# A softmax-attention stage reordered: products split around the additions, the maxima folded one unit earlier

## The chip, the cores and the metric

The kernel runs on one core of a Trainium2 chip. The metric is the time of one execution on the device in microseconds (us). Three executions of the kernel before took 3257.56, 3263.22 and 3268.09 us, median 3263.22.

## The reference, cut to what matters

One layer of an encoder is computed for two sequences, a prompt of 512 and a sample of 2048 tokens. The part in question is the attention of 8 heads, of 96 columns for queries and keys and 64 for values:

```
s = einsum('bqhd,bkhd->bhqk', q_blk, k_full) * scale
p = softmax(s, axis=-1)
o = einsum('bhqk,bkhd->bqhd', p, v)
```

Before it stand norms and projections, behind it an output projection (`w_out`) and a feed-forward part with a convolution. Everything is to be exact to about single precision.

## The kernel before, in words

Float32 products are made from float16 pairs: a value is split into a high part and a low part, and the large products are summed from pieces. `V` holds the high part, the low part and a column of ones side by side, so that one product also gives the softmax's denominator.

**Units.** The attention is cut into units. A unit of the prompt is one head and 256 queries (two blocks of 128, `nq` = 2) against 4 key tiles, in two PSUM banks; there are 16. A unit of the sample is one head and 128 queries (`nq` = 1) against 16 key tiles, in four PSUM banks of 128 keys x 512 columns (4 tiles x 128 queries); there are 128. Keys lie on the partitions. The scores of a bank stay in PSUM, rotating over seven banks; an eighth, the side bank (`psX`, one buffer, tile `x`), holds small things.

**What a unit does**, by function and line:

- `st_scores` (L939): 12 matmuls for each bank of scores on TensorE.
- `st_max` (L951, for the prompt L954 and L957): VectorE reduces a bank to the maximum over its 4 tiles, per key partition and query.
- `st_fold` (L965): VectorE folds the four banks' maxima into `mx`.
- `st_T` (L981): TensorE transposes `mx` into the side bank, in columns 384 to 512.
- `st_redT` (L989, L992, L995): VectorE reduces the transposed maxima to one per query, `m`, and splits it into a rounded part (bitwise and) and a remainder (subtract) in the small tile `p3`. These last two are called rounding and remainder here.
- `st_rep` (L1003, L1006): TensorE transposes `p3` back into the side bank (replication), ScalarE copies it with a factor of -1 into `mr` (negation).
- `st_r1` (L1015): TensorE adds the negated maxima to the scores of each bank in PSUM (the additions: four short matmuls).
- `st_exp` (L1028): ScalarE takes the exponential of each bank, with a scale `cs` per partition and a bias `ln_shift`, into `pf` (two buffers).
- `st_hi` (L1040 VectorE, L1042 ScalarE): casts of `pf` to float16, `ph`. Bank 0 on ScalarE, bank 1 on VectorE, banks 2 and 3 together on VectorE.
- `st_lo` (L1047): GpSimd subtracts, `pl = pf - ph`, one operation for each bank.
- `st_pv` (L1062, L1063): products with `V` on TensorE, a pair of matmuls for each key tile (16 pairs in a sample unit), in columns 0 to 129 of the side bank. It comes in two parts of 10 and 6 pairs (`PARTS`).
- `st_out` (L1075, L1078): ScalarE copies the sums out; each fourth time GpSimd adds high and low halves. `st_out2` (L1090, L1096): VectorE divides.

**The order** is written out by hand. The framework keeps each engine's instructions in the order of the program (a manual schedule) and sets the semaphores. For each `i` a string of letters is walked through, where `i` is the unit that is just exponentiated: scores and maxima run ahead (units `i+1`, `i+2`), products behind (`i-2`). In the sample:

```
ORDER = "r e0 A L M N P o e1 a T d f l1 b R i c h l0 l2 l3 x y z q"
```

`r` additions, `e0 e1` exponentials of banks 0 to 2 and of 3, `A P` the two parts of the products, `L` scores of bank 3 of unit `i+1`, `a b c` scores of banks 0 to 2 of unit `i+2`, `M x y z` their maxima, `N` fold of unit `i+1`, `T d R` transposes, reduction and replication of unit `i+1`, `h f i` casts, `l0` to `l3` subtractions, `o q` output. `START` and `ORDER2` are the orders for the prompt's units. There, the products go to a bank of the rotation and not to the side bank.

**Beside the units**, every fourth and the following `i` advance `prep_w_out` by one step: it loads `w_out`, finds its greatest absolute value, and splits the weights. The maximum over the partitions is made by GpSimd (`partition_all_reduce`, L840).

Of the kernel before, what the change touches and what calls it, by code (L numbers as in the profile page):

```python
# [19 lines left out]

P = 128
D = 1024
# [26 lines left out]
def encoder(ctx, tc, ins, outs, seq_names=("x_prompt", "x_sample")):  # L49
# [26 lines left out]
    dve.memset(neg_half, -0.5)  # L76
    ln_shift = small([P, 1], "ln_shift")
    dve.memset(ln_shift, LN_SHIFT)
    act.activation(small([P, 1], "warm"), ln_shift, AF.Square)

# [738 lines left out]

    def prep_w_out(raw):  # L820
# [17 lines left out]
        yield  # L838
        amr2 = raw.tile([P, 1], F32, name="amr2", bufs=1)
        pool.partition_all_reduce(amr2, am2[:, 16:17], channels=P, reduce_op=bass_isa.ReduceOp.max)  # L840
        yield
# [51 lines left out]
    with tp("pB", 2) as pB, tp("psX", 1, "right", space=PSUM) as psX, \  # L893
# [49 lines left out]
        def st_max(i, b):  # L943
            u = units[i]
            w = u["w"]
            t0, t1 = u["banks"][b]
            st = u["st"][b]
            if t1 - t0 == 4:
                if b == 0:
                    u["mx4"] = pB.tile([P, 4, P], F32, name=f"mx4_{i}", tag="mx4")  # L950
# [16 lines left out]
        def side_tile(i):  # L967

            if ("x", i) not in state:
                state["x", i] = psX.tile([P, 512], F32, name=f"x_{i}", tag="x")  # L970
            return state["x", i]

        def st_T(i):
            u = units[i]
            xp = side_tile(i - 1)
            old = units[i - 1 - LAG]["nq"] if i > LAG else 1
            u["alone"] = u["nq"] > 1 or old > 1
            u["mrp"] = xp[:, 512 - u["w"]:] if u["alone"] else xp[:, 129:129 + P]
            xp = u["xp"] = xp[:, 512 - u["w"]:]
            for j in range(u["nq"]):  # L980
                pe.matmul(xp[:, j * P:(j + 1) * P], u["mx"][:, j * P:(j + 1) * P], ident, is_transpose=True,  # L981
                          start=u["alone"], stop=True, skip_group_check=True)

        def st_redT(i):
# [3 lines left out]
            m = mc[:, 0:nq]  # L988
            dve.tensor_reduce(m, u["xp"][:, :nq * P].rearrange("p (j k) -> p j k", j=nq), axis=AX.X, op=ALU.max)  # L989
            hi, lo = p3[:, 0:nq, :, 0], p3[:, 0:nq, :, 1]  # L990
# [3 lines left out]
            for j in range(nq):  # L994
                dve.tensor_scalar(out=lo[:, j], in0=mb[:, j], scalar1=p3[:, j, 0, 0:1], scalar2=None,  # L995
                                  op0=ALU.subtract)

        def st_rep(i):
# [3 lines left out]
            for j in range(nq):  # L1002
                pe.matmul(u["mrp"][:, j * P:(j + 1) * P], p3[:, j].rearrange("p a b -> p (a b)"), ident,  # L1003
                          is_transpose=True, start=u["alone"], stop=True, skip_group_check=True)
            mr = pB.tile([P, 256], F32R, name=f"mr2_{i}", tag="mr2")
# [25 lines left out]
        def st_hi(i, b):  # L1031
# [4 lines left out]
            c = cols(u, b)  # L1036
            if b == 2 and len(u["banks"]) == 4:
                c = slice(c.start, cols(u, 3).stop)
            if b in (1, 2):
                dve.tensor_copy(u["ph"][:, c], u["pf"][:, c])  # L1040
            elif b == 0:
                act.activation(u["ph"][:, c], u["pf"][:, c], AF.Copy)  # L1042
# [59 lines left out]

        NU = len(units)
        prep = prep_w_out(pB)
        LAG = 2
        PARTS = [0, 10, 16]
        ps_first = {}
# [11 lines left out]
        def some(fn, k, bs):  # L1119
            if 0 <= k < NU:  # L1120
                for b in bs:
# [7 lines left out]
            e1=lambda i: some(st_exp, i, [3]),  # L1129
            A=lambda i: run(st_pv, i - LAG, 0),  # L1130
            P=lambda i: run(st_pv, i - LAG, 1),
            
            L=lambda i: some(st_scores, i + 1, [3]),
# [4 lines left out]
            u=lambda i: some(st_scores, i + 3, [1]),  # L1138
            v=lambda i: some(st_max, i + 3, [0]),
            w=lambda i: some(st_max, i + 3, [1]),  # L1140
# [4 lines left out]
            N=lambda i: run(st_fold, i + 1),  # L1145
            f=lambda i: some(st_hi, i, [1]),
            h=lambda i: some(st_hi, i, [0]),
            i=lambda i: some(st_hi, i, [2]),
            l0=lambda i: some(st_lo, i, [0]),
# [5 lines left out]
            R=lambda i: run(st_rep, i + 1),  # L1155
            o=lambda i: run(st_out, i - LAG),
            q=lambda i: run(st_out2, i - LAG - 1))
        START = ["a b x y", "a b T d t x u y R", "r e T d t R x y u f l1 h l0",
                 "r e T d t R x y u f l1 h l0", "r e T d A P R x y f l1 h l0 o q"]
        ORDER2 = "r e T d a b x R f l1 y h A P q o l0 c z"  # L1160
        ORDER = "r e0 A L M N P o e1 a T d f l1 b R i c h l0 l2 l3 x y z q"
        for i in range(-2, NU):
            whole = units[min(max(i, 0) + 1, NU - 1)]["nq"] == 1
            for x in (START[i + 2] if i + 2 < len(START) else ORDER if whole else ORDER2).split():
                step[x](i)
# [7 lines left out]
        todo = [(0, 0), (0, 1), (1, 0), (1, 1), (0, 2), (1, 2), (0, 3), (1, 3)]  # L1173
        for i in range(NU, NU + LAG):
            for part in range(2):
                run(st_pv, i - LAG, part)
            run(st_out2, i - LAG - 1)
            run(st_out, i - LAG)
            m = i - NU
# [4 lines left out]
            if m == LAG - 1:  # L1184
                st_out2(NU - 1)
            for x in range(3 * m + 2, 3 * m + 5):
                list(split_w_out(x))
            for t, m in todo[:4]:
                c_mm2(t, m)
            del todo[:4]  # L1190
# [531 lines left out]
```

## Time and profile before

| what | value |
|---|---|
| median of 3 runs (lowest, highest) | 3263.22 us (3257.56, 3268.09) |
| the profiled execution's own time | 3256.74 us |
| its span, first to last instruction | 3254.9 us |
| mean granted clock of TensorE | 0.978 of full speed |
| busy: TensorE, VectorE, ScalarE, GpSimd | 94%, 66%, 43%, 27% of the span |
| first and last additions (L1015) | 358.8 and 1268 us |

Times inside the profile count from the span's first instruction. PE is TensorE's matmul, PEld its weight load, DVE VectorE, ACT ScalarE, POOL GpSimd. A row of the timeline gives start, duration, engine, line, operation, output and inputs, shapes, count, and in brackets the engine's idle time ahead of it and what ended that. A matmul's duration contains its way through the array; the next one begins before it ends. A mark as L1015 is a line of the kernel before.

### The profile page before, as it was taken

How to read it: one execution, taken by the hardware profiler on the slowest of the kernel's cores; microseconds unless marked ns; L12 is line 12 of the kernel's file. 1: busy time of each engine (PE TensorE's matmuls, PEld its weight loads, DVE VectorE, ACT ScalarE, POOL GpSimd, SP SyncE). 2: the span in 40 equal slices, each digit the busy share in tenths (PEclk: the TensorE clock that was granted, in tenths of full speed). 3: DMA queues.
4: the chain of work that ended last, by engine and by line, in shares of the span. 5: the costliest groups of instructions: out<-in, count | busy, mean ns of one | idle time of the engine just before them, and what ended most of it. 6: DMA issues, size and time to landing. Idle time of an engine off the chain costs nothing. (4 is left out here: it accounts for less than half of the span.)

```text
span 3254.9 us, 59928 instructions
## 1 busy us (share of the span) xinstructions
PE 3044.8 (94%) x24601; PEld 1959.7 (60%) x24601; DVE 2161.2 (66%) x4783; ACT 1400.4 (43%) x2863; POOL 875.7 (27%) x825
## 2 busy tenths in 40 slices
PE   6999888888887888999999999999999999999998
PEld 4777577777776776444555555555545555555554
DVE  6677788788887887335777777734357666674333
ACT  4554556556565665223333333433333333333333
POOL 1211467777776775221000000000100000000000
PEclk9999899999998999999999999999999999999999
DMA  3333221201110102576111111311161111113112
GB/s 133 105 108 92 72 50 34 70 5 24 31 22 8 28 4 75 190 220 168 45 47 40 40 39 40 112 36 36 57 150 40 51 41 39 40 38 102 42 38 75
DMA packets 272061, 210.37 MB, mean 65 GB/s; under 512 B 48739, under 2 KB 247722, under 8 KB 271530
## 3 DMA queue, kind: packets, MB, share of 16 engines
q1 hardware_dynamic: 270012, 200.23, 21.1%
q0 software_dynamic: 1440, 5.24, 0.4%
q8 instruction: 193, 3.16, 0.4%
q10 hardware_dynamic: 334, 1.06, 0.1%
q14 instruction: 82, 0.67, 0.1%
HBM read 140.51 MB, written 55.38 MB: 60 GB/s over the span
## 5 line engine op out<-in xcount | busy, mean ns | idle before, releaser
L1288 PE MATMUL up<-h,ws 128*128 128x512 f16 (+1 forms) x6336 | 1146.6, 344 | 7.3 <-DMA h<-h_x_sample 5.9
L1288 PEld LDWEIGHTS <-ws 128*128 128x128 f16 x6336 | 619.9, 98 | 533.3 <-issue 6.1
L1047 POOL TENSOR_TENSOR pl<-pf,ph 128x512 f16<-128x512 f32 x544 | 660.6, 1242 | 239.9 <-DVE ph L1040 197.0
L1387 PE MATMUL dn<-G,wds 128*128 128x512 f16 (+1 forms) x3168 | 579.0, 344 | 0.0
L939 PE MATMUL st<-Q,K 96*128 96x128 f16 (+1 forms) x6336 | 469.4, 225 | 3.3 <-ACT pf L1028 2.1
L1387 PEld LDWEIGHTS <-wds 128*128 128x128 f16 x3168 | 310.0, 98 | 254.2
L939 PEld LDWEIGHTS <-K 96*128 96x128 f16 x6336 | 420.9, 102 | 14.7 <-issue 3.8
L1028 ACT ACTIVATE pf<-st,ln_shift,cs 128x512 f32<-128x512 f32 x544 | 392.7, 774 | 56.6 <-PE st L1015 47.0
L951 DVE TENSOR_REDUCE mx<-st 128x128 f32<-128x512 f32 x512 | 329.3, 684 | 70.3 <-PE st L939 69.5
L1293 ACT ACTIVATE c<-up,ctab 128x511 f32<-128x511 f32 (+3 forms) x264 | 182.1, 699 | 407.4 <-PE up L1288 401.0
L1294 DVE SCALAR_TENSOR_TENSOR c<-up,ctab,c 128x510 f32<-128x510 f32 (+3 forms) x264 | 173.5, 657 | 185.7 <-ACT c L1293 183.0
L1062 PE MATMUL x<-V,ph 128*128 128x129 f16 x2072 | 238.4, 232 | 0.4 <-ACT t L1075 0.4
L1063 PE MATMUL x<-V,pl 128*128 128x65 f16 x2072 | 228.9, 202 | 6.6 <-POOL pl L1047 6.6
L1062 PEld LDWEIGHTS <-ph 128*128 128x128 f16 x2176 | 211.3, 105 | 32.3 <-issue 32.2
L1063 PEld LDWEIGHTS <-pl 128*128 128x128 f16 x2176 | 207.2, 103 | 7.7 <-POOL pl L1047 7.3
L1394 DVE SCALAR_TENSOR_TENSOR yt<-dn,yscB,yt 128x512 f32<-128x512 f32 (+1 forms) x48 | 31.5, 660 | 227.5 <-ACT yt L1393 217.7
L1297 DVE SCALAR_TENSOR_TENSOR c<-up,ctab,c 128x511 f32<-128x511 f32 (+1 forms) x264 | 174.7, 662 | 9.3
L1006 ACT ACTIVATE mr<-x 128x128 fp32r<-128x128 f32 (+1 forms) x143 | 41.2, 288 | 276.0 <-PE x L1003 276.0
L130 ACT ACTIVATE ws<-wr,sF 128x1024 f16<-128x1024 f32 x88 | 96.2, 1138 | 147.0 <-DVE sF L1265 142.0
L1335 POOL PARTITION_ALL_REDUCE imrA<-imxA x2 | 0.7, 374 | 576.9 <-DVE imxA L1333 576.9
L1262 POOL PARTITION_ALL_REDUCE war<-wam x22 | 7.8, 356 | 527.0 <-DVE wam L1260 520.6
L1415 POOL TENSOR_TENSOR y<-y,fng 128x512 f32<-128x512 f32 (+1 forms) x42 | 45.3, 1083 | 384.4 <-ACT yp L1406 349.7
(410 smaller groups left out, 3716.4 us busy)
## 6 DMA issues: line engine op xcount, KB each, us to landing
wr<-in_w_up SPq DMA_DIRECT2D x88, 512.0 KB, 4.9
wd<-in_w_down SPq DMA_DIRECT2D x32, 512.0 KB, 4.3
x_s<-in_x_sample SPq DMA_DIRECT2D x8, 1024.0 KB
xt_Cs<-in_x_sample SPq DMA_DIRECT2D x8, 1024.0 KB, 7.8
x_x_sample<-xt_Cs SPq DMA_DIRECT2D x8, 1024.0 KB, 4.0
h_x_sample<-rows_Cs SPq DMA_DIRECT2D x16, 512.0 KB, 2.7
wd<-in_w_down SPq DMA_DIRECT2D x16, 384.0 KB, 3.5
y<-x_x_sample SPq DMA_DIRECT2D x3, 2048.0 KB, 8.7
```

The source lines that it names most:

```text
L130: act.activation(hi, src, AF.Identity, scale=scale)
L939: pe.matmul(st[:, (t - t0) * w:(t - t0 + 1) * w], kt[:, x, t * P:(t + 1) * P], qt[:, y, u["q0"]:u["q0"] + w], start=n == 0 and t == t0, st ...
L951: dve.tensor_reduce(u["mx4"][:, b, :], st.rearrange("p (t q) -> p q t", q=w), axis=AX.X, op=ALU.max)
L1028: act.activation(u["pf"][:, c], u["st"][b][:, :c.stop - c.start], AF.Exp, bias=ln_shift[:, 0:1], scale=cs[:, 0:1])
L1047: pool.tensor_tensor(out=u["pl"][:, c], in0=u["pf"][:, c], in1=u["ph"][:, c], op=ALU.subtract)
L1062: pe.matmul(op[:, j, 0:129], u["ph"][:, c0:c0 + P], V[:, k0 + t, h, 0:129], start=t == 0, stop=False)
L1063: pe.matmul(op[:, j, 64:129], u["pl"][:, c0:c0 + P], V[:, k0 + t, h, 64:129], start=False, stop=t == nkt - 1)
L1288: pe.matmul(ps[:, :ncol], ws[side][:, k, x, :], ht[:, k, y, :ncol], start=m == 0, stop=m == 3 * KT - 1)
L1293: act.activation(c[:, :n], ps[:, :n], AF.Identity, scale=cw[:, 1, col:col + 1], bias=ctab[:, 3, col:col + 1])
L1294: dve.scalar_tensor_tensor(out=c[:, 1:n], in0=ps[:, 0:n - 1], scalar=cw[:, 0, col:col + 1], in1=c[:, 1:n], op0=ALU.mult, op1=ALU.add)
L1297: dve.scalar_tensor_tensor(out=c[:, 0:j1], in0=ps[:, 1:1 + j1], scalar=cw[:, 2, col:col + 1], in1=c[:, 0:j1], op0=ALU.mult, op1=ALU.add)
L1387: pe.matmul(acc[part][:, :n], w[f // 8][:, f % 8, x, :], G_[0][:, f, y, o:o + n], start=f in (0, NF - 1) and (x, y) == (0, 0), stop=f >= N ...
```

## The change

The sample's unit is reordered, and with it what the side bank holds. The diff, cut to its core:

```diff
-    ln_shift = small([P, 1], "ln_shift")
-    dve.memset(ln_shift, LN_SHIFT)
...
-        pool.partition_all_reduce(amr2, am2[:, 16:17], channels=P, reduce_op=bass_isa.ReduceOp.max)
+        pm = side()[0:1, 256:384]
+        pe.matmul(pm, am2[:, 16:17], ident, is_transpose=True, start=False, stop=True, skip_group_check=True)
+        m1 = raw.tile([1, 1], F32, name="m1", bufs=1)
+        dve.tensor_reduce(m1, pm, axis=AX.X, op=ALU.max)
+        yield
+        pm = side()[:, 256:257]
+        pe.matmul(pm, m1.to_broadcast([1, P]), ident[:1, :1], is_transpose=True, ...)
+        dve.tensor_copy(amr2, pm)
...
+        shift = pB.tile([P, 1], F32, name="shift", bufs=1)
+        dve.reciprocal(shift, cs)
+        dve.tensor_scalar(out=shift, in0=shift, scalar1=LN_SHIFT, scalar2=None, op0=ALU.mult)
...
-                dve.tensor_reduce(u["mx4"][:, b, :], st.rearrange("p (t q) -> p q t", q=w), axis=AX.X, op=ALU.max)
+                dve.tensor_reduce(u["mx2"] if b == 3 else u["mx3"][:, :, b], st.rearrange("p (t q) -> p q t", q=w),
+                                  axis=AX.X, op=ALU.max)
...
-                dve.tensor_reduce(u["mx"][:, 0:P], u["mx4"].rearrange("p b q -> p q b"), axis=AX.X, op=ALU.max)
+                dve.tensor_reduce(u["mx"][:, 0:P], u["mx3"], axis=AX.X, op=ALU.max)
...
+            x = state["x", i] = psX.tile([P, 512], F32, name=f"x_{i}", tag="x")
+            parts = [u["mx"][:, j * P:(j + 1) * P] for j in range(u["nq"])]
+            if u["nq"] == 1:
+                parts.append(u["mx2"])
+            u["xp"], u["mrp"] = x[:, 0:256], x[:, 512 - u["w"]:]
...
-                dve.tensor_scalar(out=lo[:, j], in0=mb[:, j], scalar1=p3[:, j, 0, 0:1], scalar2=None,
-                                  op0=ALU.subtract)
+                dve.tensor_scalar(out=lo[:, j], in0=mb[:, j], scalar1=p3[:, j, 0, 0:1], scalar2=shift[:, 0:1],
+                                  op0=ALU.subtract, op1=ALU.subtract)
...
-            act.activation(u["pf"][:, c], u["st"][b][:, :c.stop - c.start], AF.Exp, bias=ln_shift[:, 0:1],
-                           scale=cs[:, 0:1])
+            act.activation(u["pf"][:, c], u["st"][b][:, :c.stop - c.start], AF.Exp, scale=cs[:, 0:1])
...
-                op = side_tile(i + LAG) if units[min(i + LAG + 1, NU - 1)]["nq"] == 1 else bank(f"op_{i}")
+                op = state["x", i + 2] if i + 2 < NU else bank(f"op_{i}")
...
-        PARTS = [0, 10, 16]
+        PARTS = [0, 8, 16]
...
+            A=lambda i: run(st_pv, i - 1, 0),
+            B=lambda i: run(st_pv, i - 2, 1),
+            F=lambda i: run(st_fold, i + 2),
+            h0=lambda i: run(st_hi, i, 0),
+            h1=lambda i: run(st_hi, i, 1),
+            f1=lambda i: run(st_hi, i, 1, 1, dve),
+            f2=lambda i: run(st_hi, i, 2, 1, dve),
+            f3=lambda i: run(st_hi, i, 3, 1, dve),
...
-        ORDER2 = "r e T d a b x R f l1 y h A P q o l0 c z"
-        ORDER = "r e0 A L M N P o e1 a T d f l1 b R i c h l0 l2 l3 x y z q"
+        ORDER2 = "r e B o T d a b x R f1 l1 y h0 A q l0 c z F"
+        TURN = "r e B o L a M x T d b h0 f1 R y l0 l1 A c z F q"
+        ORDER = "r e0 B L o e1 a M f2 T d b c h0 R h1 l2 l0 l1 A x y z F f3 l3 q"
```

So a unit's products now come in halves of 8 pairs: `A`, behind the unit's next but one replication and into the same side tile, and `B`, behind the additions of the `i` after that. The fold `F` takes three banks and is made one `i` earlier; the fourth bank's maxima `mx2` are transposed by themselves, and the reduction runs over both transposes. `f2` and `f3` cast banks 2 and 3 on VectorE, `h0` and `h1` banks 0 and 1 on ScalarE. The exponential's shift goes into the remainder. The prompt's products go to the side bank too. `TURN` is the order of the one unit between prompt and sample, and the tail behind the last unit is written anew for the split products.

## Rows read from the trace of the kernel before

**Rows 1.** Windows: us, busy PE, PEld, DVE, ACT, POOL, PEclk, DMA share, GB/s.

```profile
358.83:424.92 66.09, 55.55 (x490) 41.75 (x490) 53.36 (x132) 39.11 (x73) 37.39 (x35) 0.85 0.36 86
444.59:1260.80 816.21, 692.78 (x10666) 602.85 (x10664) 674.20 (x1350) 481.26 (x877) 624.77 (x529) 0.95 0.11 26
```

**Rows 2.** Timeline of one sample unit, 849.8 to 856.2 us, all engines.

```profile
849.82 0.51 PE L1015 MATMUL st<-mr,ones 2*128 2x512 f32 x4
850.26 0.23 PE L1062 MATMUL x<-V,ph 128*128 128x129 f16 x1
850.42 2.12 ACT L1028 ACTIVATE pf<-st,ln_shift,cs 128x512 f32<-128x512 f32 x3 [0.36 <-PE st L1015]
...
851.11 0.19 PE L1063 MATMUL x<-V,pl 128*128 128x65 f16 x1
851.25 0.83 PE L939 MATMUL st<-Q,K 96*128 96x128 f16 x12
...
852.11 0.69 DVE L951 TENSOR_REDUCE mx<-st 128x128 f32<-128x512 f32 x1 [0.55 <-PE st L939]
...
852.63 0.28 ACT L1075 ACTIVATE t<-x 128x129 f32<-128x129 f32 x1
852.84 1.06 DVE L965 TENSOR_REDUCE mx<-mx 128x128 f32<-128x512 f32 x1
...
854.04 0.30 PE L981 MATMUL x<-ident,mx 128*128 128x128 f32 x1 [0.77 <-DVE mx L965]
854.38 0.29 DVE L989 TENSOR_REDUCE mc<-x 128x1 f32<-128x128 f32 x1 [0.49 <-PE x L981]
...
855.20 0.33 PE L1003 MATMUL x<-ident,p 128*128 128x128 f32 x1 [0.18 <-DVE p L995]
855.57 0.28 ACT L1006 ACTIVATE mr<-x 128x128 fp32r<-128x128 f32 x1 [1.99 <-PE x L1003]
855.62 4.82 POOL L1047 TENSOR_TENSOR pl<-pf,ph 128x512 f16<-128x512 f32 x4 [1.49 <-DVE ph L1040]
...
856.13 0.50 PE L1015 MATMUL st<-mr,ones 2*128 2x512 f32 x4
```

**Rows 3.** Windows: longest unit, a long one, a usual one; three, then five prompt units.

```profile
1003.88:1019.93 16.05, 8.08 (x90) 7.41 (x88) 5.18 (x11) 3.86 (x8) 9.46 (x9) 0.57 0.00 1
482.44:490.04 7.60, 6.86 (x90) 6.17 (x88) 5.17 (x11) 3.86 (x8) 4.82 (x5) 0.78 0.01 2
490.04:496.35 6.31, 5.35 (x89) 4.63 (x87) 5.17 (x11) 3.85 (x8) 5.50 (x6) 1.00 0.00 0
...
370.81:387.56 16.75, 16.75 (x102) 12.64 (x102) 10.62 (x28) 8.55 (x16) 8.73 (x8) 0.51 0.09 25
391.41:411.70 20.29, 16.53 (x172) 12.55 (x170) 18.15 (x47) 13.11 (x26) 13.25 (x12) 1.00 0.26 71
```

**Rows 4.** Groups by shape, ScalarE, whole span.

```profile
L1028 ACT ACTIVATE pf<-st,ln_shift,cs 128x512 f32<-128x512 f32 x544 | 392.7, 774 | 56.6 <-PE st L1015 47.0 <-POOL pl L1047 9.3
L1393 ACT ACTIVATE yt<-dn,yscA 128x512 f32<-128x512 f32 x32 | 21.9, 686 | 195.5 <-PE dn L1387 195.5
```

**Rows 5.** Groups by shape, VectorE, whole span.

```profile
L989 DVE TENSOR_REDUCE mc<-x 128x2 f32<-128x256 f32 x15 | 6.3, 421 | 9.6 <-PE x L981 9.6
```

**Rows 6.** Timeline of GpSimd, then of VectorE, 362.9 to 365.5 us, a prompt unit.

```profile
362.95 2.26 POOL L1047 TENSOR_TENSOR pl<-pf,ph 128x512 f16<-128x512 f32 x2 [23.37 <-DVE ph L1040]
...
363.59 0.55 DVE L992 TENSOR_SCALAR p<-mc 128x8 int32<-128x8 int32 x1
364.17 1.20 DVE L995 TENSOR_SCALAR p<-mc,p 128x4 f32<-128x4 f32 x2
```

**Rows 7.** Waits of weight loads, 450 to 1250 us: total us, times, longest.

```profile
PEld x L981 <- ACT pf L1028: 105.1, 118, 0.9
```

**Rows 8.** Timeline of TensorE, a prompt unit whose additions begin at 403.64 us.

```profile
404.49 0.41 PE L981 MATMUL x<-ident,mx 128*128 128x128 f32 x2 [0.35 <-DVE mx L954]
```

**Rows 9.** Timeline of GpSimd, 995 to 1020 us.

```profile
1001.50 0.38 POOL L840 PARTITION_ALL_REDUCE amr<-am  x1 [5.93 <-DVE mx L951]
```

More of the change, by code (lines that the diff above doesn't have):

```diff
@@ L76, in encoder @@
     dve.memset(neg_half, -0.5)
-    ln_shift = small([P, 1], "ln_shift")
-    dve.memset(ln_shift, LN_SHIFT)
-    act.activation(small([P, 1], "warm"), ln_shift, AF.Square)
+    act.activation(small([P, 1], "warm"), neg_half[:, 0:1], AF.Square)
     n_scale = [0]
@@ L818, in w_o_part, with prep_w_out @@
         return w_o[:, m, part * 512:part * 512 + 512].bitcast(F16)
-    def prep_w_out(raw):
+    def prep_w_out(raw, side):
         am2 = raw.tile([P, 17], F32, name="am2", bufs=1)
@@ L838, in prep_w_out @@
         yield
+        pm = side()[0:1, 256:384]
[4 more added lines that the diff above has]
+        pm = side()[:, 256:257]
+        pe.matmul(pm, m1.to_broadcast([1, P]), ident[:1, :1], is_transpose=True, start=False, stop=True,
+                  skip_group_check=True)
         amr2 = raw.tile([P, 1], F32, name="amr2", bufs=1)
-        pool.partition_all_reduce(amr2, am2[:, 16:17], channels=P, reduce_op=bass_isa.ReduceOp.max)
-        yield
+        dve.tensor_copy(amr2, pm)
         swo, swo_i = pow2_scale(amr2, 15)
@@ L949, in st_max @@
                 if b == 0:
-                    u["mx4"] = pB.tile([P, 4, P], F32, name=f"mx4_{i}", tag="mx4")
-                dve.tensor_reduce(u["mx4"][:, b, :], st.rearrange("p (t q) -> p q t", q=w), axis=AX.X, op=ALU.max)
+                    u["mx3"] = pB.tile([P, P, 3], F32, name=f"mx3_{i}", tag="mx3")
+                if b == 3:
+                    u["mx2"] = pB.tile([P, P], F32, name=f"mx2_{i}", tag="mx2")
+                dve.tensor_reduce(u["mx2"] if b == 3 else u["mx3"][:, :, b], st.rearrange("p (t q) -> p q t", q=w),
+                                  axis=AX.X, op=ALU.max)
             elif b:
@@ L964, in st_fold @@
                 u["mx"] = pB.tile([P, 256], F32, name=f"mx_{i}", tag="mx")
-                dve.tensor_reduce(u["mx"][:, 0:P], u["mx4"].rearrange("p b q -> p q b"), axis=AX.X, op=ALU.max)
[L967 to L971, printed above, removed]
+                dve.tensor_reduce(u["mx"][:, 0:P], u["mx3"], axis=AX.X, op=ALU.max)
         def st_T(i):
             u = units[i]
[L975 to L982, printed above, removed]
+            x = state["x", i] = psX.tile([P, 512], F32, name=f"x_{i}", tag="x")
[3 more added lines that the diff above has]
+            u["xp"], u["mrp"] = x[:, 0:256], x[:, 512 - u["w"]:]
+            for j, part in enumerate(parts):
+                pe.matmul(u["xp"][:, j * P:(j + 1) * P], part, ident, is_transpose=True, start=j == 0, stop=True,
+                          skip_group_check=True)
         def st_redT(i):
@@ L1003, in st_rep @@
                 pe.matmul(u["mrp"][:, j * P:(j + 1) * P], p3[:, j].rearrange("p a b -> p (a b)"), ident,
-                          is_transpose=True, start=u["alone"], stop=True, skip_group_check=True)
+                          is_transpose=True, start=False, stop=True, skip_group_check=True)
             mr = pB.tile([P, 256], F32R, name=f"mr2_{i}", tag="mr2")
@@ L1035, in st_hi @@
                 u["pl"] = pB.tile([P, 2048], F16, name=f"pl_{i}", tag="pl", bufs=3)
[L1036 to L1039, printed above, removed]
+            if b >= len(u["banks"]):
+                return
+            c = slice(cols(u, b).start, cols(u, b + n - 1).stop)
+            if eng is dve:
                 dve.tensor_copy(u["ph"][:, c], u["pf"][:, c])
-            elif b == 0:
+            else:
                 act.activation(u["ph"][:, c], u["pf"][:, c], AF.Copy)
@@ L1103, in encoder @@
         NU = len(units)
-        prep = prep_w_out(pB)
-        LAG = 2
-        PARTS = [0, 10, 16]
+        prep = prep_w_out(pB, lambda: state["x", max(k for n, k in (x for x in state if x[0] == "x"))])
+        PARTS = [0, 8, 16]
         ps_first = {}
@@ L1138, in encoder @@
             u=lambda i: some(st_scores, i + 3, [1]),
-            v=lambda i: some(st_max, i + 3, [0]),
-            w=lambda i: some(st_max, i + 3, [1]),
             M=lambda i: some(st_max, i + 1, [3]),
@@ L1144, in encoder @@
             z=lambda i: some(st_max, i + 2, [2]),
[L1145 to L1148, printed above, removed]
+            F=lambda i: run(st_fold, i + 2),
[4 more added lines that the diff above has]
+            f3=lambda i: run(st_hi, i, 3, 1, dve),
             l0=lambda i: some(st_lo, i, [0]),
@@ L1155, in encoder @@
             R=lambda i: run(st_rep, i + 1),
[L1156 to L1159, printed above, removed]
-        ORDER2 = "r e T d a b x R f l1 y h A P q o l0 c z"
-        ORDER = "r e0 A L M N P o e1 a T d f l1 b R i c h l0 l2 l3 x y z q"
+            o=lambda i: run(st_out, i - 2),
+            q=lambda i: run(st_out2, i - 3))
+        START = ["a b x y", "a b T d t x u y R", "r e T d t R x y u f1 l1 h0 l0",
+                 "r e T d t R x y u f1 l1 h0 l0 A", "r e B o T d R x y f1 l1 h0 l0 A"]
+        ORDER2 = "r e B o T d a b x R f1 l1 y h0 A q l0 c z F"
+        TURN = "r e B o L a M x T d b h0 f1 R y l0 l1 A c z F q"
+        ORDER = "r e0 B L o e1 a M f2 T d b c h0 R h1 l2 l0 l1 A x y z F f3 l3 q"
         for i in range(-2, NU):
-            whole = units[min(max(i, 0) + 1, NU - 1)]["nq"] == 1
-            for x in (START[i + 2] if i + 2 < len(START) else ORDER if whole else ORDER2).split():
+            now, then = (units[min(max(k, 0), NU - 1)]["nq"] for k in (i, i + 1))
+            order = START[i + 2] if i + 2 < len(START) else ORDER if now == 1 else TURN if then == 1 else ORDER2
+            for x in order.split():
                 step[x](i)
@@ L1173, in encoder @@
         todo = [(0, 0), (0, 1), (1, 0), (1, 1), (0, 2), (1, 2), (0, 3), (1, 3)]
[L1174 to L1179, printed above, removed]
+        st_pv(NU - 2, 1)
+        st_pv(NU - 1, 0)
+        st_out(NU - 2)
+        st_pv(NU - 1, 1)
+        st_out(NU - 1)
+        for m in range(2):
             if m == 1:
@@ L1187, in encoder @@
                 list(split_w_out(x))
-            for t, m in todo[:4]:
-                c_mm2(t, m)
+            for t, k in todo[:4]:
+                c_mm2(t, k)
             del todo[:4]
```

7 lines of the change are left out of this document (2 added, 5 removed).

## The prediction

> **What bounds the kernel now.** The page's busy shares put TensorE at 94%, but a share over the whole span says little of a stage, and the change touches only the attention, some 909 of 3255 us. So I first cut the span into stretches [rows 1]: the prompt's 16 units take 66.1 us, the sample's 124 units from 444.59 to 1260.80 us take 816.2. Nearly every one of these takes 6.31 us, the distance of two groups of additions (849.82 and 856.13 in [rows 2]). 124 x 6.31 = 782; the other 34 us are 9.7 us in one unit and some 1.3 us in each of 18 others, of which [rows 3] shows one of each.
>
> Then I read one unit in order of time [rows 2]. No engine is full: GpSimd works 4.82 of 6.31 us, and TensorE stands still for 0.77 us until the fold releases the transposes. The unit is one chain: additions (849.82), first exponential (850.42), which frees the bank for the scores of bank 3 (851.25), their maxima (852.11), the fold (852.84, 1.06 us), transposes (854.04), reduction of what they give (854.38), replication (855.20), negation on ScalarE (855.57), the next additions (856.13). To be seen as well: GpSimd pauses for 1.49 us ahead of 855.62, and the reduction and the two small operations behind it on VectorE lie in just that pause.
>
> **The change, step by step,** counting from a unit's additions, with the durations of [rows 2] unless another group is named.
>
> *Exponentials without bias.* The exponential of 128x512 takes 774 ns with two operands per partition; a ScalarE operation of that shape with one takes 686 [rows 4]. Three begin every 0.67 us (2.12 for three), so now every 0.59: the first ends at 0.60 + 0.69 = 1.29 (now 1.37), the third at 2.46. The copy of the sums (0.28) follows at +0.1 and ends at 2.84. Bounds: no gain, if the program supplies a bias operand anyway, and 0.09 per exponential; I take 0.09, after the row. (At the other bound all that follows is 0.1 us later, 12 us in all.) The shift rides on the remainder's instruction and adds none.
>
> *Products split around the additions.* B, 8 of 16 pairs at 0.088 (the first of 10 pairs begins at 850.26, the last matmul of the tenth at 851.11), runs from 0.44 to 1.14. The scores of bank 3 begin at 1.34, their maxima at +0.86 = 2.20, and end at 2.89.
>
> *Fold ahead.* The fold of three banks is made a unit earlier, so 1.06 us leave the chain. It costs a second transpose (0.14, as from transpose to scores) and a reduction over 256 columns, 421 ns instead of 290 [rows 5]. The transposes wait for the copy (2.84) and the maxima (2.89): 3.0 instead of 4.2. The new fold, 1.06 us at most, costs nothing: behind the maxima of bank 2 VectorE has nothing to do until 2.2 of the next unit, and needs 1.5 at most for fold and cast. The cast of bank 1 goes to ScalarE (0.62), behind the negation, where ScalarE waits for the next additions anyway.
>
> *The cast of bank 2 between maxima and reduction.* It runs from 2.84 to 3.26 while the transposes run, and the reduction begins at 3.36, so it costs no time itself. But it releases the first subtraction on GpSimd, at about 3.35, inside the reduction. What that does stands in [rows 6]: GpSimd subtracts from 362.95 for 2.26 us, two in a row. VectorE's rounding of the maxima, ready at 363.59, takes 0.55 instead of 0.17 and ends 0.03 after the first subtraction; the remainder, ready at 364.17, ends behind the second (two take 1.20, where one takes 0.23). These small operations do not run beside a subtraction; each waits for the end of the one in progress. Now the chain meets just that: the subtraction of bank 2 lasts 3.35 to 4.50, rounding ends at 4.53; bank 0, whose cast on ScalarE is done at 3.75, follows from 4.46 to 5.61; the remainder ends at 5.64. Without the hold it would end at 4.45, before the last scores leave TensorE (4.7). So replication moves from 4.7 to 5.72: **1.0 us per unit.** The new remainder subtracts two operands per partition, a form that no row shows. Between free (replication at 4.85) and held (5.72) I take held, after the row with one operand, which it is nearest to. [...]
>
> *The products wait for the negation.* A now follows replication into the same PSUM tile that ScalarE reads for the negation. Does TensorE wait there for columns that do not overlap? The transposes' weight load waits on ScalarE 118 times [rows 7], though all that it reads comes from VectorE; only the copy of the sums, from other columns of the same tile, can be meant. So yes: replication 5.72, negation 6.09 to 6.37, A 6.43 to 7.20 (8 pairs and 0.07, as between scores and additions now), next additions **7.20**. Behind it nothing else is late: ScalarE's last cast is done at 6.9, GpSimd's bank 1 runs from 7.0, bank 3 behind its cast at 1.2 of the next unit, ended by 2.4.
>
> Against 6.31 that is +0.89, over 124 units **+110 us.**
>
> *TensorE's clock.* [...] A unit of now pauses for 0.77 us before the transposes and 0.18 before the replication. The new one pauses from the last scores (4.7) to A (6.43), 1.6 us without the replication, so I expect falls in many units. Bounds: none (0) and one in each unit (+1.3). Between them the rows show this: with a pause of 0.77 us in each unit 18 of 124 units of the sample were slow, and the prompt, whose units at full clock stand still for 0.75 us (20.29 less 16.53, over five units), was slow for 16.75 of its 66.09 us. The new unit stands still for twice as long as either (7.20 less 5.35 and 0.15 for the added transpose: 1.7). I take 0.6 per unit, in the upper half of the bounds: 124 x 0.6 x 1.3 = 97, less the 18 x 1.3 = 24 of now: **+73 us.** [...]
>
> *The prompt's units.* Transposes now stand 0.35 us behind TensorE's last work, held by maxima alone [rows 8], some 0.85 behind the additions. New: B, two exponentials (0.60 to 1.87), the copy of 128x258 (0.38), transposes at 2.2. The period becomes about 5.3 instead of 4.06: 14 x 1.2 = 17, less the 3 x 1.5 = 5 of today's slow units, +12 at full clock; with all units slow by 1.5, +33. I take **+25,** since these units now pause longest of all.
>
> *GpSimd's reduction over partitions* stands at 1001.50 behind a pause of 5.93 us [rows 9]; the unit that begins next takes 16.05 instead of 6.31 [rows 3]. Two transposes and a small reduction replace it; TensorE waits for VectorE's queue, under 1 us each: -9.7 + 2 = **-8.** The tail keeps its work: 0.
>
> **Sum:** 110 + 73 + 25 - 8 = +200 us. Against the profiled execution's own 3256.7 us that is 3457; the median of the runs shown is 0.2% above it, so I predict **3463 us.**
>
> **Rivals.** (1) *The clock stays up:* all as above without new falls, -97 in the sample and -13 in the prompt: 3353 (with today's falls 3377). For it: in the sample the clock always came back within a unit. 0.21. (2) *A does not wait for the negation:* it runs meanwhile and the additions follow at 6.66: 124 x 0.35 = 43, prompt +12 to +25, falls as now, -8: 3310 to 3325. For it: the columns do not overlap; against it [rows 7]. 0.14. (3) *The subtraction does not hold the small operations:* replication at 4.7, unit 6.03. 124 x -0.28 = -35, falls halved -12, -8, prompt +25: 3233. It decides if GpSimd begins later than 4.4, when VectorE is through with them. Against it: the cast ends at 3.26 and GpSimd has nothing else to do. 0.12. (4) *Neither wait:* unit 5.5, 124 x -0.81 = -100, no falls -24, -8, prompt +20: 3151. 0.06.
>
> The forecast has 0.47. Its own range, from 0.3 to 0.9 falls per unit and the prompt's bounds, is 3400 to 3520; a fall in every unit gives 3555. The range over it and the cases (1) and (2), 3280 to 3560, leaves out (3) and (4), 0.18. A difference under 0.3% (10 us) could not be told from none. Slower: 0.47 + 0.21 + 0.14, less a little = 0.80; within 0.3%: 0.03, the upper end of (3) or the lower of (2); faster 0.17.
>
> **What would show it.** In the profile after: additions 7.2 us apart or more; rounding and remainder at about 0.7 and 1.1 us instead of 0.17 and 0.23, ending with a subtraction; first products released by the negation; PEclk of 7 to 9 in the attention's slices; exponentials at 0.69; no reduction over partitions at 1000 us. Wrong if the small operations keep 0.2 us, if products start 0.2 us after replication, or if the additions stand under 6.3 apart.

## The result, and the profile after

The changed kernel takes **3463.9 us** (median of 4 runs, 3458.7 to 3473.5) against 3260.4 before: a ratio of 1.063, with an interval of 1.059 to 1.067. 3463 us were forecast. The profiled execution is the longest of the four, 3473.5 us with a span of 3471.5, 217 us over that of before. A sum that comes out right can still be made of terms that are wrong, so it is taken apart here.

Windows of the changed kernel over the same units as in [rows 1], the prompt (from the first group of additions to the sixteenth, which is 15 units, in [rows 1] too, where the prediction speaks of 16) and the sample (124 units); the columns are us, busy PE, PEld, DVE, ACT, POOL, PEclk, DMA share, GB/s:

```profile
357.43:461.07 103.64, 82.89 (x498) 57.45 (x499) 48.35 (x133) 36.08 (x73) 38.24 (x36) 0.54 0.26 57
485.09:1472.87 987.78, 806.84 (x10793) 692.36 (x10792) 793.41 (x1352) 486.91 (x1000) 591.53 (x528) 0.87 0.09 22
```

The prompt lost 37.6 us (66.09 before), the sample 171.6 (816.21 before). The three units between them lost 4.4, and all the rest of the span 3. VectorE worked 119 us longer in the sample (674 before), although the fold became shorter: instructions there last longer, and the next lines show which. The granted clock went from 0.95 to 0.87 in the sample, and from 0.85 to 0.54 in the prompt.

Timeline of one sample unit of the changed kernel at full clock, to be read beside [rows 2]:

```profile
819.75 0.51 PE L1022 MATMUL st<-mr,ones 2*128 2x512 f32 x4
...
820.35 1.84 ACT L1035 ACTIVATE pf<-st,cs 128x512 f32<-128x512 f32 x3 [0.91 <-PE st L1022]
...
821.95 0.69 DVE L961 TENSOR_REDUCE mx<-st 128x128 f32<-128x512 f32 x1 [1.00 <-PE st L947]
...
822.56 0.42 DVE L1046 CAST ph<-pf 128x512 f16<-128x512 f32 x1
...
822.87 1.50 PE L947 MATMUL st<-Q,K 96*128 96x128 f16 x24
823.06 2.26 POOL L1053 TENSOR_TENSOR pl<-pf,ph 128x512 f16<-128x512 f32 x2 [0.86 <-DVE ph L1046]
823.07 0.42 DVE L996 TENSOR_REDUCE mc<-x 128x1 f32<-128x256 f32 x1
823.52 0.72 DVE L999 TENSOR_SCALAR p<-mc 128x4 int32<-128x4 int32 x1
824.28 1.07 DVE L1002 TENSOR_SCALAR p<-mc,p,shift 128x4 f32<-128x4 f32 x1
...
825.41 0.33 PE L1010 MATMUL x<-ident,p 128*128 128x128 f32 x1 [1.04 <-DVE p L1002]
...
825.77 0.28 ACT L1013 ACTIVATE mr<-x 128x128 fp32r<-128x128 f32 x1 [2.32 <-PE x L1010]
...
826.10 0.22 PE L1068 MATMUL x<-V,ph 128*128 128x129 f16 x1 [0.37 <-ACT mr L1013]
...
826.89 0.51 PE L1022 MATMUL st<-mr,ones 2*128 2x512 f32 x4
```

Follow the chain. The maxima of bank 3 end at 822.64, so the last transpose runs at 2.95 us of the unit instead of 4.22: the fold has left the chain, as planned. Then the cast of bank 2 ends at 822.98, GpSimd begins to subtract at 823.06, and VectorE, whose rounding is ready at 823.52, ends it only at 824.24, when the first of two subtractions is over; the remainder, ready at 824.28, ends at 825.35, with the second. TensorE waits 1.04 us for it. Then the products wait for the negation, another 0.37. The unit is 7.14 us long.

Groups by shape on VectorE from 490 to 1240 us:

```profile
L1002 DVE TENSOR_SCALAR p<-mc,p,shift 128x4 f32<-128x4 f32 x95 | 101.6, 1069 | 3.5
L1046 DVE CAST ph<-pf 128x512 f16<-128x512 f32 x188 | 90.9, 483 | 0.0
L999 DVE TENSOR_SCALAR p<-mc 128x4 int32<-128x4 int32 x94 | 61.9, 659 | 3.2
...
L1102 DVE TENSOR_TENSOR o<-t,ri 128x256 f32<-128x256 f32 x24 | 31.6, 1318 | 2.7 <-DVE ri L1096 0.5
```

The same operations in the kernel before, in the same window:

```profile
L995 DVE TENSOR_SCALAR p<-mc,p 128x4 f32<-128x4 f32 x113 | 26.1, 231 | 4.0
L992 DVE TENSOR_SCALAR p<-mc 128x4 int32<-128x4 int32 x113 | 19.8, 176 | 3.8
L1096 DVE TENSOR_TENSOR o<-t,ri 128x256 f32<-128x256 f32 x28 | 12.2, 437 | 2.7
```

Two lines of the waits from 485 to 1472 us (us in total, times, longest):

```profile
PE x L1010 <- DVE p L1002: 121.0, 116, 1.6
...
PE x L1068 <- ACT mr L1013: 44.9, 123, 0.4
```

So the unit above is the rule: rounding takes 0.66 us on average (0.18 before), the remainder 1.07 (0.23), and the first products wait for the negation in 123 of 124 units. The last line of the first list (L1102) is one that the prediction does not speak of: the product that finishes the outputs of every fourth unit takes 1.32 us where it took 0.44.

The next unit of the same timeline holds a second thing that was missed:

```profile
829.57 0.73 POOL L1084 TENSOR_TENSOR t<-t 128x256 f32<-128x256 f32 x1 [0.24 <-ACT t L1081]
829.70 0.89 DVE L1046 CAST ph<-pf 128x512 f16<-128x512 f32 x1
...
830.73 2.26 POOL L1053 TENSOR_TENSOR pl<-pf,ph 128x512 f16<-128x512 f32 x2 [0.43 <-DVE ph L1046]
```

In every fourth unit GpSimd adds the two halves of the sums, and this addition now falls on the cast of bank 2 and holds it (0.89 us instead of 0.42). The subtractions begin 0.5 us later, and rounding and remainder end later with them: this unit takes 7.66 us.

The prompt, in a timeline of one of its units (additions at 416.52, the next at 423.88):

```profile
417.40 1.26 ACT L1035 ACTIVATE pf<-st,cs 128x512 f32<-128x512 f32 x2 [1.16 <-PE st L1022]
...
418.56 0.39 ACT L1081 ACTIVATE t<-x 128x258 f32<-128x258 f32 x1
...
418.99 0.69 PE L988 MATMUL x<-ident,mx 128*128 128x128 f32 x2 [0.92 <-ACT t L1081]
```

The transposes wait for the copy of the sums, and that stands behind two exponentials. In [rows 8] only maxima held them, for 0.35 us.

### The profile page after: what moved, and what is told of

Its sections match the earlier page's. It is cut to its first block, busy times and chain, and to the rows that moved or that the text cites. A ratio compares the mean times of both kernels' runs of the same rounds, so it can differ in the third digit from the quotient of the medians.

```text
span 3471.5 us, 60351 instructions
## 1 busy us (share of the span) xinstructions
PE 3197.0 (92%) x24731; PEld 2071.8 (60%) x24731; DVE 2277.6 (66%) x4786; ACT 1403.0 (40%) x2991; POOL 840.1 (24%) x824
## 3 DMA queue, kind: packets, MB, share of 16 engines
q10 hardware_dynamic: 334, 1.06, 0.1%
## 5 line engine op out<-in xcount | busy, mean ns | idle before, releaser
L1053 POOL TENSOR_TENSOR pl<-pf,ph 128x512 f16<-128x512 f32 x544 | 624.0, 1157 | 478.5 <-DVE ph L1046 290.6
L947 PE MATMUL st<-Q,K 96*128 96x128 f16 (+1 forms) x6336 | 491.1, 243 | 3.1 <-DVE ms_s L133 1.2
L947 PEld LDWEIGHTS <-K 96*128 96x128 f16 x6336 | 458.1, 110 | 22.2 <-issue 1.8
L1035 ACT ACTIVATE pf<-st,cs 128x512 f32<-128x512 f32 x544 | 346.5, 690 | 160.1 <-PE st L1022 158.9
L1068 PE MATMUL x<-V,ph 128*128 128x129 f16 x2144 | 277.7, 245 | 54.5 <-ACT mr L1013 52.9
L1069 PE MATMUL x<-V,pl 128*128 128x65 f16 x2144 | 270.5, 216 | 0.0
L1068 PEld LDWEIGHTS <-ph 128*128 128x128 f16 x2176 | 238.9, 116 | 44.1 <-issue 44.0
L1048 ACT ACTIVATE ph<-pf 128x512 f16<-128x512 f32 x272 | 173.2, 637 | 0.0
L1010 PE MATMUL x<-ident,p 128*128 128x128 f32 x160 | 52.8, 350 | 126.7 <-DVE p L1002 126.3
L133 DVE SCALAR_TENSOR_TENSOR wds<-wd,fs,wds 128x128 f16<-128x128 f32 x352 | 113.7, 380 | 51.5 <-ACT wds L128 51.5
```

The source lines that it names most:

```text
L947: pe.matmul(st[:, (t - t0) * w:(t - t0 + 1) * w], kt[:, x, t * P:(t + 1) * P], qt[:, y, u["q0"]:u["q0"] + w], start=n == 0 and t == t0, st ...
L1053: pool.tensor_tensor(out=u["pl"][:, c], in0=u["pf"][:, c], in1=u["ph"][:, c], op=ALU.subtract)
L1068: pe.matmul(op[:, j, 0:129], u["ph"][:, c0:c0 + P], V[:, k0 + t, h, 0:129], start=t == 0, stop=False)
L1069: pe.matmul(op[:, j, 64:129], u["pl"][:, c0:c0 + P], V[:, k0 + t, h, 64:129], start=False, stop=t == nkt - 1)
```

## The experiments

Each was timed beside the kernel before, with 4 or 5 executions of its own. Medians of the kernel before on the same chips: 3254.9 us for the first four, 3250.4 for the next four, 3252.2 for the last.

**The cast moved behind the remainder.**

```diff
-        ORDER = "r e0 B L o e1 a M f2 T d b c h0 R h1 l2 l0 l1 A x y z F f3 l3 q"
+        ORDER = "r e0 B L o e1 a M T d f2 b c h0 R h1 l2 l0 l1 A x y z F f3 l3 q"
```

> The changed kernel with one step moved: VectorE casts bank 2 behind the remainder, not ahead of the reduction, so that GpSimd has no subtraction in progress while VectorE rounds. Theory (a subtraction in progress holds the two small operations): rounding 0.17 us instead of 0.63, the remainder about 0.25 instead of 1.04, the replication right behind the last scores at 4.65 us of the unit (5.66 in the changed kernel), a unit of about 6.15 us at full clock instead of 7.13: 127 x 0.98 = 124 us less, and with the pause gone most of the clock's 0.85 us per unit too. 3250 to 3340 us against 3464. Rival 1 (the new form of the remainder, with two operands per partition, is slow by itself): rounding 0.17, remainder still near 1.0, replication 0.5 us earlier at most, unit 6.7, some 3400 us. Rival 2 (the unit is long for another reason): unit still above 7 us, 3450 or more.

Measured: **3233.4 us**, 0.9935 of before (0.9913 to 0.9957). Window of its 124 sample units:

```profile
480.49:1238.63 758.14, 689.13 (x10792) 589.95 (x10790) 638.87 (x1352) 487.02 (x1000) 615.53 (x528) 1.00 0.11 28
```

Its groups on VectorE from 480 to 1240 us:

```profile
L1002 DVE TENSOR_SCALAR p<-mc,p,shift 128x4 f32<-128x4 f32 x124 | 36.0, 290 | 4.5
...
L999 DVE TENSOR_SCALAR p<-mc 128x4 int32<-128x4 int32 x124 | 29.5, 238 | 4.3
```

One step moved in an order of 27 is worth 230 us: the changed kernel becomes 0.65% faster than the one before. The remainder with two operands takes 0.29 us when nothing holds it, so rival 1 falls. The usual unit is 5.88 us, and the mean of the 124 is 6.11, about the 6.15 expected. The gain is beyond the expected range all the same. The 6.15 was set against 7.13, the usual unit, but at full clock the mean unit of the changed kernel is 7.45 us (the run with filler, below): 1.33 us less in each of 124 units are 165 us instead of the 124 expected. The other 64 us are the lower clock, which is gone (1.00).

**The products ahead of the replication.**

```diff
-        ORDER = "r e0 B L o e1 a M f2 T d b c h0 R h1 l2 l0 l1 A x y z F f3 l3 q"
+        ORDER = "r e0 B L o e1 a M f2 T d b c h0 A R h1 l2 l0 l1 x y z F f3 l3 q"
```

> The changed kernel with one step moved: the first half of the products (A) stands ahead of the replication on TensorE, not behind it; rounding and remainder stay held. Theory (A waits for the negation, since both touch one PSUM tile): A begins right behind the last scores at 4.65 us of the unit instead of 6.35, lies beside the held remainder, and the additions follow the negation at about 6.4 us: unit 6.4 at full clock instead of 7.13, 127 x 0.73 = 93 us less, and part of the falls of the clock with it: 3290 to 3380 us. Rival (A comes late because its remainders from GpSimd or its casts are late): A still begins after 5.6 us of the unit, unit 7 us or more, 3440 us or more.

Measured: **3329.3 us**, 1.0225 (1.0189 to 1.0261). Timeline of one unit (additions at 821.87):

```profile
824.68 0.69 DVE L1046 CAST ph<-pf 128x512 f16<-128x512 f32 x1
...
825.45 2.27 POOL L1053 TENSOR_TENSOR pl<-pf,ph 128x512 f16<-128x512 f32 x2 [0.36 <-DVE ph L1046]
825.73 0.90 DVE L999 TENSOR_SCALAR p<-mc 128x4 int32<-128x4 int32 x1
826.32 0.22 PE L1068 MATMUL x<-V,ph 128*128 128x129 f16 x1
...
826.67 1.07 DVE L1002 TENSOR_SCALAR p<-mc,p,shift 128x4 f32<-128x4 f32 x1
...
827.80 0.33 PE L1010 MATMUL x<-ident,p 128*128 128x128 f32 x1 [0.61 <-DVE p L1002]
...
828.50 0.51 PE L1022 MATMUL st<-mr,ones 2*128 2x512 f32 x4 [0.37 <-ACT mr L1013]
```

The products begin at 4.45 us of the unit, right behind the scores, so nothing but the negation had kept them. The additions still come at 6.63 instead of the 6.4 expected: in this unit GpSimd's last subtraction of the unit before has slid onto the cast (0.69 us), and the hold begins and ends 0.27 us later. By their place in a group of four the median units are 6.63, 5.99, 6.63 and 7.62 us, the last one with the finishing product. The gain of 135 us can't be added to the 230 of the late cast: they come to more than the whole loss, and each holds some of the lower clock (granted here: 0.97).

**Work that nobody reads, in TensorE's pause.**

```diff
+            D=lambda i: run(st_fill, i + 1),
+        def st_fill(i):
+            u = units[i]
+            kt, qt = loaded[(u["s"]["base"], u["h"])]
+            for n in range(15):
+                pe.matmul(state["x", i][:, 258:384], kt[:, 0, 0:P], qt[:, 0, u["q0"]:u["q0"] + 126], start=False,
+                          stop=True, skip_group_check=True)
-        ORDER = "r e0 B L o e1 a M f2 T d b c h0 R h1 l2 l0 l1 A x y z F f3 l3 q"
+        ORDER = "r e0 B L o e1 a M f2 T d b c h0 D R h1 l2 l0 l1 A x y z F f3 l3 q"
```

> The changed kernel with 15 more matmuls of 126 columns per sample unit on TensorE, in the pause between the last scores and the replication; nobody reads what they give. They measure what the granted clock costs by itself. Theory (the unit is 7.13 us at full clock, and the mean of 7.98 is the lower clock that follows the pauses): PEclk near 1.0 over the sample's units, unit 7.13 to 7.2, 127 x 0.8 = 100 us less: about 3365 us, although TensorE has more to do. Rival (the clock falls for the 0.4 us pause ahead of A as well, or the long units have another cause): PEclk stays near 0.8, units 8 us or more, 3460 us or more.

Measured: **3404.2 us**, 1.0460 (1.0430 to 1.0491). Window of its 124 sample units:

```profile
489.01:1412.60 923.59, 818.31 (x12654) 703.97 (x12652) 812.49 (x1352) 487.66 (x1000) 592.16 (x528) 0.99 0.09 23
```

Two lines of its timeline, in a unit whose additions are at 913.67, the next at 921.30:

```profile
914.95 1.16 POOL L1060 TENSOR_TENSOR pl<-pf,ph 128x512 f16<-128x512 f32 x1 [0.36 <-DVE ri L1103]
...
915.06 1.32 DVE L1109 TENSOR_TENSOR o<-t,ri 128x256 f32<-128x256 f32 x1
```

1860 more matmuls, and the 124 units are 64.2 us shorter: that is about what the lower clock costs the changed kernel, less than the 100 expected. The miss teaches something. At full clock the units are not all 7.13 us long: by their place in a group of four the medians are 7.13, 7.63, 7.13 and 7.67. The lines above show the one with the finishing product, which is held until 916.11, before the maxima of bank 3 can run; the other is the one with GpSimd's addition. Their half microseconds had been taken for a lower clock.

**The prompt in the order of before.** C makes all products of the unit before last, in a bank of their own; the orders of the first units and of the turn to the sample are changed likewise.

```diff
-        ORDER2 = "r e B o T d a b x R f1 l1 y h0 A q l0 c z F"
+        ORDER2 = "r e T d a b x R f1 l1 y h0 C q o l0 c z F"
```

> The changed kernel, but its 16 prompt units keep the order of the kernel before (all products of a unit together, into a bank of their own, so that transposes do not wait for the copy of the sums behind the exponentials). Theory (the prompt's loss is that wait, and the low clock that follows from its pauses): the 16 units take about 66 us again instead of 110.8, the sample's units are as in the changed kernel: 45 us less, about 3420 us. Rival (the prompt is slow from the low clock alone, however it is ordered): the units stay near 7 us at a clock of 0.5, under 15 us less, 3450 us or more.

Measured: **3426.4 us**, 1.0526 (1.0489 to 1.0562). Window of the prompt:

```profile
355.48:421.36 65.88, 57.37 (x491) 42.29 (x492) 53.58 (x132) 36.44 (x73) 37.42 (x35) 0.82 0.38 88
```

The loss of 37.6 us is gone (66.09 before), and with it most of the low clock (0.82, 0.85 before). The sample's units are as in the changed kernel (988.7 us). The 45 us expected were a slip: 110.8 us hold sixteen units, 66 us hold fifteen. The run takes two waits away together, that of the transposes for the copy and that of the products for the negation (0.47 us in each prompt unit of the changed kernel), so it does not tell them apart.

**The hold, in the kernel before.** This is the reverse test: nothing of the change but a cast and its subtraction ahead of the reduction.

```diff
-        ORDER = "r e0 A L M N P o e1 a T d f l1 b R i c h l0 l2 l3 x y z q"
+        ORDER = "r e0 A L M N P o e1 a T f l1 d b R i c h l0 l2 l3 x y z q"
```

> The kernel before with one step moved: the cast of bank 1 (VectorE) and the subtraction that it releases stand ahead of the reduction of the transposes, where VectorE waits for TensorE for 0.49 us, instead of behind the remainder. All else (products, fold, exponentials, prompt) is as before. Theory (a subtraction in progress holds the small operations, in any order of the rest): the subtraction begins about 0.1 us behind the reduction's start, rounding is held to its end (about 0.85 us instead of 0.17), the remainder may stay free since the next cast comes only behind the replication; unit 6.9 to 7.0 us instead of 6.31 at full clock, 127 x 0.65 = 83 us more, and up to 60 more for falls of the clock in the longer pause: 3335 to 3400 us against 3255. Rival (what made the changed kernel's small operations long belongs to its new forms or its new order, not to a subtraction): rounding stays at 0.17, unit 6.31 or a little less, as GpSimd begins earlier: 3240 to 3260 us.

Measured: **3410.8 us**, 1.0490 (1.0458 to 1.0523). Timeline of one unit (additions at 803.33, the next at 810.79):

```profile
808.36 1.15 POOL L1047 TENSOR_TENSOR pl<-pf,ph 128x512 f16<-128x512 f32 x1 [1.15 <-DVE ph L1040]
808.37 0.29 DVE L989 TENSOR_REDUCE mc<-x 128x1 f32<-128x128 f32 x1
808.69 0.85 DVE L992 TENSOR_SCALAR p<-mc 128x4 int32<-128x4 int32 x1
809.58 0.23 DVE L995 TENSOR_SCALAR p<-mc,p 128x4 f32<-128x4 f32 x1
```

Two steps moved in the kernel before make it 160 us slower, with the rounding at 0.85 us, as expected, and the remainder free, as expected. The whole is 11 us over the range. The usual unit is 6.92 us at full clock, as expected, but two in four are longer: 7.25 where GpSimd's addition holds the cast (0.67 us), and 7.46 where the finishing product is held as well (1.24 us on average).

**Four combinations.** All have the prompt of before and the cast behind the remainder; the four orders stand as their expectations do.

```diff
-        ORDER = "r e0 B L o e1 a M f2 T d b c h0 R h1 l2 l0 l1 A x y z F f3 l3 q"
+        ORDER = "r e0 B L o e1 a M T d f2 b h0 A R h1 l2 l0 l1 c x y z F f3 l3 q"
...
+        ORDER = "r e0 B L o e1 a M q T d f2 b c h0 R h1 l2 l0 l1 A x y z F f3 l3"
...
+        ORDER = "r e0 B L o e1 a M q T d f2 b h0 A R h1 l2 l0 l1 c x y z F f3 l3"
...
+        ORDER = "r e0 B L o e1 a M T d q f2 b h0 A R h1 l2 l0 l1 c x y z F f3 l3"
```

> The changed kernel with the prompt's units as in the kernel before, the cast of bank 2 behind the remainder, and on TensorE the first products (A) ahead of the replication and the scores of the last bank behind it, beside the negation. Theory (the changed kernel's loss is the hold of the small operations, the wait of A for the negation, the clock that falls in these pauses, and the prompt's wait for the copy of the sums): TensorE has no pause left but those of the unit's start, unit 5.7 to 5.9 us at full clock, few falls, prompt about 72 us to the first sample unit: 127 x (6.59 - 5.9) = 88 us less than before, 8 for the reduction over partitions: 3130 to 3180 us. Rival (GpSimd, with 4.7 us of work and a quiet window of over 1 us per unit, becomes the bound and its subtractions fall on the rounding of the next unit): unit 6.2 us or more, 3200 us or more.

> The run with the late cast, with the prompt's units as in the kernel before, and the finishing of the outputs (reciprocal and product of every fourth unit on VectorE) moved from the unit's end, where a subtraction holds it to 1.1 us and the maxima of bank 3 wait behind it, to just behind these maxima, where VectorE waits for the transposes. TensorE's order is that of the changed kernel, with A behind the negation. Theory: units of 5.88 us where every fourth took 6.32, 12 us less, and 38 us less in the prompt: 3233 - 50 = 3183 us (3170 to 3200). Rival (the hold of that product is hidden): 3195 us, units of 6.32 as before.

> Both of the last two: products ahead of the replication, last scores behind it, late cast, finishing of the outputs behind the maxima of bank 3, prompt as in the kernel before. Theory: the gains add, unit 5.6 to 5.8 us, 3110 to 3165 us. Rival (GpSimd's 4.7 us and its quiet window are the bound by then): no faster than the better of the two.

> The first combined run (products ahead of the replication, last scores behind it, late cast, prompt as in the kernel before), with the finishing of the outputs of every fourth unit put between the remainder and the late cast, the only stretch of VectorE in which no subtraction is in progress and TensorE does not wait for it. Theory (these units are long because a subtraction holds that product and the maxima of bank 3 come late): the product takes 0.43 us instead of 1.1, the units of 6.3 us become about 5.5, 31 x 0.8 = 25 us less: about 3147 us. Rival (GpSimd then begins its subtractions 0.6 us later, ends later, and holds the rounding of the next unit): the gain is given back, 3162 to 3175 us.

Measured: 3171.5 us, 0.9758 (0.9732 to 0.9784); 3189.2, 0.9814 (0.9788 to 0.9839); 3167.3, 0.9741 (0.9713 to 0.9769); **3165.5, 0.9731 (0.9716 to 0.9746)**. The first, third and fourth can't be told apart; each beats both kernels. Window of the 124 sample units of the first:

```profile
441.33:1175.89 734.56, 675.20 (x10792) 591.99 (x10790) 649.13 (x1352) 486.73 (x1001) 615.30 (x528) 1.00 0.12 29
```

The same of the fourth:

```profile
440.81:1169.45 728.64, 683.51 (x10792) 592.51 (x10790) 648.52 (x1352) 486.79 (x1001) 607.84 (x528) 1.00 0.12 29
```

Two groups of the fourth from 480 to 1150 us:

```profile
L999 DVE TENSOR_SCALAR p<-mc 128x4 int32<-128x4 int32 x113 | 47.7, 422 | 3.9
...
L1102 DVE TENSOR_TENSOR o<-t,ri 128x256 f32<-128x256 f32 x28 | 11.9, 426 | 3.1 <-DVE ri L1096 0.5
```

A mean unit of 5.92 and 5.88 us (6.58 before). The first run came inside its range, if with a unit just over the 5.7 to 5.9 expected. Moving the finishing product out of the hold was worth little, twice. In the second it stayed among GpSimd's subtractions in part, and its units kept 6.33 us: the rival held there, although the whole lies in the theory's range. Of its 44 us against the late cast, 35 are the prompt's (101.33 to 65.88). In the fourth the product is free (0.43 us), and its units go from 6.33 to 6.01; but GpSimd then begins later, ends later, and holds the next unit's rounding (0.42 us on average), so the shortest units grow from 5.40 to 5.53. Some 6 of the 25 us expected are left, within what the two intervals allow: the time lies in the rival's range, not at the theory's 3147 us. In the third the gains did not add: 3167 us, no better than the first, as its rival said. With 4.7 us of subtractions per unit and a stretch of about 1 us in which GpSimd waits to begin them (539.2 and 111.5 us over 114 units of the fourth), a unit of 5.9 us has little room left.

## Why the prediction was right

**The sum against the parts.** The terms of the prediction, beside what the windows give (124 units of 6.31 us are 782.4):

| term | predicted | measured | from |
|---|---|---|---|
| longer unit at full clock | +110 | +141 | 923.6 (run with filler) - 782.4 |
| lower clock, sample | +73 | +40 | 987.8 - 923.6, less the 24 of before |
| prompt | +25 | +38 | 103.64 - 66.09 |
| reduction over partitions | -8 | -10 | the 9.7 of before; what replaces it lies in the 141 |
| rest | 0 | +7 | three units between the stages 4, elsewhere 3 |
| sum | +200 | +217 | profiled executions; the medians differ by 204 |

The forecast case came true in sign and mechanism. That the sum fits to some us is luck: three terms were off by 13 to 33 us, and the two largest errors, +31 and -33, cancelled.

*The chain.* Times from a unit's additions, predicted and (from the timeline) measured: end of the cast 3.26 and 3.23, start of the subtraction 3.35 and 3.31, end of rounding 4.53 and 4.49, end of the remainder 5.64 and 5.60, replication 5.72 and 5.66, first products 6.43 and 6.35, next additions 7.20 and 7.14. Each of its two causes has a run that takes it away: with the cast behind the remainder the usual unit is 5.88 us, with the products ahead of the replication 6.63. The hold also has a run that puts it where it had not been.

*What was mis-sized in the steady term.* "Behind it nothing else is late" failed. It was said of the usual unit, and every second unit has something else: GpSimd's addition of the halves (0.73 us), ahead of the late cast, or the finishing product on VectorE, which now meets a subtraction. The usual unit gave 9 us back (124 by 7.13 instead of 7.20), so 40 us are to be explained: 62 such units by 0.52 us are 32, and single units make up the rest.

*What was mis-sized in the clock.* 0.6 falls per unit by 1.3 us is 0.78 us per unit; 64.2 / 124 = 0.52 were measured. The price was right and the number too high: the trace of the changed kernel has 51 falls of the granted clock from 1.0 to 0.5 of full speed in the 124 units (18 before), 0.41 per unit, and 64.2 us over 51 falls are 1.26 us each. That there would be falls at all was read from the rows of before, where 16 of the 18 slow units follow no pause of TensorE over 0.78 us. The prediction passed over one long pause, though: in the unit at 1003.88 TensorE stood still for 6.65 us behind GpSimd's reduction, and that unit (clock 0.57) and the two after it were slow. In the 124 units of the changed kernel the longest pause of TensorE is 1.6 us, and the clock was 0.87.

*The prompt.* The wait that was forecast is there: the transposes wait for the copy behind two exponentials. The size lay above even the upper bound of +33: the units ran almost wholly at the lower clock (0.54), where the usual one takes 7.37 us, not the 5.3 + 1.5 of the bound (the 1.5 is 16.75 / 3 less 20.29 / 5 of [rows 3], units at a granted clock of 0.51 and of 1.00). No run shows these units at full clock, so how the 38 us divide between the two waits and the clock stays open.

*Edits costed at little.* The exponential takes 690 ns (774 before, 686 forecast). The two transposes that replace GpSimd's reduction fall in two units, of 8.94 and 7.87 us: they hold TensorE for 0.8 us each, and the 16.05 of before is gone.

*The rivals.* (1), that the clock stays up, fell with 0.87. (2), that the products do not wait for the negation, fell with 123 waits in 124 units; 3329.3 us, the run in which the order keeps them from waiting, lies near what it forecast (3310 to 3325). Products and negation use different columns of one tile, and the products still wait for the negation (0.37 us in the unit shown, 44.9 us in all). But the waits are semaphores that the framework sets, so no run shows what the chip would do without them. A bank of its own for the negation was not tried: at that point of the unit the other seven hold scores. (3), that a subtraction holds nothing, fell with rounding and remainder, and (4) with (2) and (3). What (3) forecast, 3233 us, is what the run with the late cast takes, with the remainder free and the rounding nearly so (0.24 us); that it fits to the us is coincidence.

## What to carry to other kernels

When an operation is moved, ask what it releases and what that will run beside: here the cast itself was free, and the subtraction that it started 1.4 us earlier (3.31 instead of 4.67 us into the unit) cost 230 us. If VectorE and GpSimd both work in a unit, as here (rounding 0.66 us on average in the changed kernel and 0.24 with the late cast, the remainder 1.07 and 0.29), the small VectorE operations on the critical chain need a stretch in which GpSimd has nothing to run, and the order of GpSimd's releases is the way to make one. Look at every unit of a period, not at the usual one: what happens once in four units also meets a new neighbour.

## What the runs showed of the hardware

*Which VectorE operations a subtraction on GpSimd holds.* Rounding (0.17 us free, up to 0.96 held), remainder (0.29 and 1.07), casts (0.42, and 0.69 beside a subtraction or 0.89 beside GpSimd's addition) and the product with two inputs (0.43 and 1.32) are held; reductions are not: the fold of the kernel before takes 1.06 us beside a subtraction (115 units) and away from one (9), the shorter fold of the changed kernel 0.55 beside one (all 124 units), and the maxima there 0.68 either way (292 and 204 of them). Over the sample units of the changed kernel but the first, both small operations always overlap a subtraction, and they end a median of 29 ns after one.

*Two queued subtractions take turns with VectorE.* In 127 of 128 sample units of the changed kernel rounding got in between the first and the second, and the remainder, ready 0.04 us later in the unit shown, had to wait out the whole second one: in these units the second of the two small operations ended only with the second subtraction (a median of 29 ns behind it).

*TensorE's clock.* Fifteen matmuls per unit whose results nobody reads made the kernel 60 us faster (3463.9 to 3404.2), by a granted clock of 0.99 instead of 0.87 over the sample. The 51 falls of the changed kernel came with pauses of 1.0 to 1.6 us for the remainder and of 0.37 us for the negation in units at full clock; in the run with the late cast, where TensorE waits for the negation 124 times (45.3 us, up to 0.4) and for the remainder hardly at all (0.3 us in all), the clock stayed at 1.00.
